# A list-scheduled order of all queues, from a first pass that notes the program as a graph, in a two-layer hybrid encoder step

## The chip, the cores and the metric

The kernel runs on one core of one Trainium2 chip. The metric is the device time of one execution in microseconds (us); less is better. Every execution starts with its inputs in the chip's memory (HBM) and ends with its outputs there. All arithmetic is in float32; the large matrix products are made of three products of float32r parts (a high and a low part of each operand), small ones are plain float32.

## What is computed

The reference is one inference step of a streaming encoder trunk with two layers on 512 prompt tokens and 32 sample tokens, 1024 features each. Cut to what matters:

```python
for layer in range(2):
    x = post_norm(x, 0.5 * swiglu(x, ffn_up[layer, 0], ffn_down[layer, 0]), ...)   # 1024 -> 2 x 2816 -> 1024
    if layer == 0:
        y, st = mixer_ab(x, ...)     # gated linear recurrence (RG-LRU) beside retention, 4 heads of 128
    else:
        y, st = mixer_c(x, ...)      # RWKV-7 time mixing, 16 heads of 64
    x = post_norm(x, y, ...)
    x = post_norm(x, cross_attn(x, mem_k[layer], mem_v[layer], xa_q[layer], xa_o[layer]), ...)  # 4 heads, 256 rows of memory
    x = post_norm(x, 0.5 * swiglu(x, ffn_up[layer, 1], ffn_down[layer, 1]), ...)
# post_norm(x, sub) = layer_norm(ALPHA * x + sub); the memory's keys and values are outputs too, and the mixers' states
```

RWKV-7's recurrence, the part that the prediction turns on, updates a 64 x 64 state of each head once per token:

```python
def step(S, inp):
    r_t, w_t, k_t, v_t, kk_t, b_t = inp
    sa = jnp.einsum('bhvk,bhk->bhv', S, -kk_t)
    S = S * w_t[:, :, None, :] + sa[..., None] * b_t[:, :, None, :] + v_t[..., None] * k_t[:, :, None, :]
    return S, jnp.einsum('bhvk,bhk->bhv', S, r_t)
```

## The kernel before

**Tiling.** The 544 tokens are two halves, A (256 prompt tokens) and B (256 prompt tokens and the 32 of the sample). A half stays in SBUF through all layers, with features on the partitions: `X` is the half itself, `XH` and `XL` its high and low parts, `HH` and `HL` those of an intermediate result (the names in the profile end in A or B). Weights come from HBM in granules of 1024 x 128 (512 KB) into one of three buffers `wr`. ScalarE makes the high part of a granule in one of five slots `W`, and VectorE or GpSimd the low part; `linear` then runs 24 matmuls of 128 x 128 weights against the half's 256 or 288 columns into one PSUM bank (`mm`). Four banks are called `mm` and four `ax`. In the feed-forward layers a granule serves both halves; from somewhat before the second layer's mixer until after its attention (`SOLO`) each half loads its own granules, so that one half's products can fill the other's waits.

**The recurrence** (`wkv` and the five tasks that it starts, in the second layer's mixer) works on nine blocks of 64 tokens (the last has 32), in chunks of 32. For every block:
- `wkv_prep` computes decays and keys. Its first instruction is a product on GpSimd (`K.gtt`, into `arena`), its second the square of that on ScalarE, its third a matmul with the matrix `bones`. It ends with a store of a triangular matrix N to HBM (`dn`).
- `wkv_solve` loads N in another layout (`P<-dn`, 512 KB, a head and chunk and a quarter of the rows to a partition), and inverts I + N in 31 steps of two GpSimd instructions (in the profile `P<-LC,P` and `LC<-LC,P`). It stores the inverse (`dz<-LC`) and loads it in a third layout (`W<-dz`), two of four loads by SP's queue and two by ScalarE's.
- `wkv_load` transposes, `wkv_chain` takes the state through the block's chunks, and `wkv_norm` norms and gates what comes out: a matmul with `cent`, four GpSimd products and sums on `HL`, and more.

**What sets the order.** Each engine takes its instructions from a queue, in order, and so does each issuer of DMAs (mostly SP; ScalarE and GpSimd for a few). The order of the queues comes about in two stages:
- A planner inside the kernel. The tasks of the program are Python generators. `Kern.run` lets go on the one that can go on first by an estimated time; each instruction passes through `Kern.plan`, and `Clock.op` says at what estimated time it starts, from durations written in the helpers (`mm`, `_v`, `gtt`, `act`, `dma`) and from when its operands are written and free. Tasks with a band under 0 (the recurrence's, the norms') see only each other's instructions as taken time; a band over 0 comes after everything. The estimated times also decide which buffer, slot or bank is taken next, and `ett` puts a subtraction on VectorE or on GpSimd, whichever the estimate has done first (the weights' low parts ask GpSimd to be 300 ns ahead).
- The framework's scheduler. `plan` hands each instruction's estimated start on as its priority. At the end the framework runs the program against its own timing model (`schedule_with_timeline_sim=True`), and whenever an engine is free in that model, the instruction of the lowest priority value among those that are ready is put next in its queue.

`place_tables` then goes through ScalarE's finished queue and puts in the loads of its function tables.

The lines that the profile names most: L395 is the matmul of `mm`, L400 the transpose of `tr`, L408 VectorE's `tt`, L412 GpSimd's `gtt`, L486 the activation of `act`, L491 the start of a DMA, L2049 a table load.

Of the kernel before, what the change touches and what calls it, by code (L numbers as in the profile page):

```python
# [3 lines left out]

# [42 lines left out]
MEM_FILL = 28  # L47
LOG_G = np.log1p(-(2.0 ** (-5.0 - np.arange(4, dtype=np.float32)))).astype(np.float32)
# [54 lines left out]
class Res:  # L103
    """Things that are taken and given back, with the times from which they are free."""
# [27 lines left out]
class Line:  # L132
    """The spans of time in which an engine is taken; a later comer may fill a gap."""
# [28 lines left out]
class Clock:  # L162
    """An estimate of when instructions run, in ns: what an engine does and what its operands wait for.
    It orders the emission and the engines' queues, and nothing else rests on it."""
# [35 lines left out]
    def renew(self, old, new):  # L200
        """A tile takes over the room of an older one."""
# [46 lines left out]

class Arena:
# [26 lines left out]
    def top(self, n):  # L276
        """The last n elements."""
# [50 lines left out]
class Arenas:  # L328
    """Several arenas as one."""
# [44 lines left out]
class Kern(Clock):  # L374
    def __init__(self, tc, ins, outs, consts, stages):
        super().__init__()
        self.tc, self.nc, self.i, self.o, self.c = tc, tc.nc, ins, outs, consts
# [6 lines left out]
    def plan(self, eng, dur, outs, ins, queue=None):  # L384
        s = self.op(eng, dur, outs, [t for t in ins if t is not None and not isinstance(t, (int, float))], self.band, queue)
        self.tc.cur_priority = 10000000 + int(s) + self.band * (BAND if self.band > 0 else 0000)

    def mm(self, out, lhsT, rhs, start=True, stop=True):
# [6 lines left out]
        self.nc.tensor.matmul(out, lhsT, rhs, start=start, stop=stop)  # L395

    def tr(self, out, in_, k0=0):
        k = in_.shape[0]
        self.plan("pe", 109.0, [out], [in_])
        self.nc.tensor.transpose(out, in_, self.ident[k0:k0 + k, k0:k0 + k])  # L400

    def _v(self, out, ins, fast=False):
        fast = fast and all(t.space != PSUM for t in ins)
        self.plan("v", 70 + free_size(out) / (1.92 if fast else 0.96), [out], ins)

    def tt(self, out, a, b, op=ALU.mult):
        self._v(out, [a, b])
        self.nc.vector.tensor_tensor(out, a, b, op=op)  # L408

    def gtt(self, out, a, b, op=ALU.mult):  # L410
        self.plan("g", 150 + free_size(out) * 2.0, [out], [a, b])
        self.nc.gpsimd.tensor_tensor(out, a, b, op=op)  # L412

    def ett(self, out, a, b, op=ALU.mult, lag=0.0):
        """On the engine that is through first; GpSimd has to be ahead by some ns."""
# [5 lines left out]
        dv, dg = 70 + n / 0.96, 150 + n * 2.0  # L421
# [8 lines left out]
    def stt(self, out, a, s, b, op0, op1):  # L430
        self._v(out, [a, b])
        self.nc.vector.scalar_tensor_tensor(out, a, s, b, op0=op0, op1=op1)  # L432

    def ts(self, out, a, s1, s2=None, op0=ALU.mult, op1=None):
        self._v(out, [a], True)
        if op1 is None:
            self.nc.vector.tensor_scalar(out, a, s1, None, op0=op0)
        else:
            self.nc.vector.tensor_scalar(out, a, s1, s2, op0=op0, op1=op1)

    def vcopy(self, out, a):
        self._v(out, [a], True)
        self.nc.vector.tensor_copy(out, a)

    def memset(self, out, v):
        self._v(out, [])
        self.nc.vector.memset(out, v)

    def gmemset(self, out, v):
        self.plan("g", 50 + free_size(out) * 0.83, [out], [])  # L450
        self.nc.gpsimd.memset(out, v)

    def scan(self, out, a, b, ini):
        self._v(out, [a, b])
        self.nc.vector.tensor_tensor_scan(out, a, b, ini, op0=ALU.mult, op1=ALU.add)

    def rmax(self, out, a):
        self._v(a, [a])
        self.nc.vector.reduce_max(out, a, axis=mybir.AxisListType.X)

    def recip(self, out, a):
        self._v(out, [a])
        self.nc.vector.reciprocal(out, a)

    def bn(self, out, tmp, a):
        self._v(a, [a])
        self.nc.vector.bn_stats(tmp, a)
        self._v(out, [tmp])
        self.nc.vector.bn_aggr(out, tmp)

    def act(self, out, a, f=AF.Copy, bias=None, scale=1.0, accum=None):
        dur = (60 if a.space == PSUM else 100) + free_size(out) / 1.2
        dur += 93 * ((bias is not None and not isinstance(bias, float)) + (not isinstance(scale, float)))
        sets = TABLES.get(f)
        if sets and self.set not in sets:
            self.set = sets[0]
            dur += 1283
        self.plan("a", dur, [out] if accum is None else [out, accum], [a])
# [7 lines left out]
        return self.nc.scalar.activation(out, a, f, bias=bias, scale=scale, **kw)  # L486

    def dma(self, out, a, queue="sync"):
        n = 4 * int(np.prod(out.shape))
        self.plan("dma", n / 350 + 60, [out], [a], queue)  # L490
        getattr(self.nc, queue).dma_start(out, a)  # L491
# [7 lines left out]
    def sigmoid(self, out, a, bias=None, half=None):  # L499
        """1 / (1 + exp(-a - bias)) = (1 + tanh((a + bias) / 2)) / 2; half: bias / 2."""  # L500
# [66 lines left out]
    def lend(self, slots, raws):  # L567
        """Slots and buffers of the weights for another use."""
# [9 lines left out]
    def stream(self, granules, after=(), limit=None, first=0):  # L578
        """Granules that are loaded one after another, from when the streams before them are through."""
# [1508 lines left out]
```

## Time and profile before

| | |
|---|---|
| time, median of 3 runs (lowest, highest) | 3021.44 us (3020.57, 3023.30) |
| the profiled execution, first to last instruction | 3028.7 us |
| TensorE busy, matmuls | 2833.4 us, 22456 |
| VectorE / ScalarE / GpSimd busy | 1743.4 / 1276.8 / 830.1 us |
| mean granted TensorE clock | 0.945 |
| from HBM, to HBM | 313.09 MB, 13.92 MB |

The profiled execution has no separate time without its profile; its span is 7.3 us over the median of the runs, and the shares of the page refer to that span. PE stands for TensorE's matmuls, PEld for its weight loads, DVE for VectorE, ACT for ScalarE, POOL for GpSimd, SP for the engine that only starts DMAs; a `q` behind a name means the engine's sequencer. A matmul's duration is longer than the distance to the next one, since matmuls are pipelined. A wait is shown with the engine that waited, its instruction, and who ended the wait.

### The profile page before, as it was taken

To read this page: it belongs to the slowest core of one execution; us is meant where nothing else is said; L and a number is where in the kernel's file an instruction comes from. 1 tells how busy PE (TensorE), PEld (TensorE's weight loads), DVE (VectorE), ACT (ScalarE), POOL (GpSimd) and SP (SyncE) were. 2 spreads that over 40 slices of the span, in tenths; PEclk is the share of its full clock that TensorE was granted. 3 is DMA by queue.
4 is the path that set the end of the run, shared out by engine and by line. 5 is a ranking of instruction groups with operands and counts; after the bars stand their busy time and mean duration, and the time that the engine had idled before them with its cause. 6 is when DMAs were issued, how large, how long until landed. Compare 5 with 4: busy or idle time off the path is not lost.

```text
span 3028.7 us, 54637 instructions
## 1 busy us (share of the span) xinstructions
PE 2833.4 (94%) x22456; PEld 2716.3 (90%) x22456; DVE 1743.4 (58%) x3099; ACT 1276.8 (42%) x2184; POOL 830.1 (27%) x1088
## 2 busy tenths in 40 slices
PE   9999998998999999999999898888878889999998
PEld 8999998998998999989999897776767779998997
DVE  5333337677767333365355756674675666767655
ACT  4223233665545222234244343343435455655544
POOL 2001104333313000032011212466375543422301
PEclk9999999999999999999999998788778879999999
DMA  6443443322332232322356453122223135645563
GB/s 182 126 119 115 130 119 97 88 68 81 98 98 84 85 90 84 89 87 77 90 155 179 120 168 106 39 65 62 69 73 87 49 98 174 177 141 157 169 176 93
DMA packets 626331, 330.56 MB, mean 109 GB/s; under 512 B 45480, under 2 KB 620160, under 8 KB 626080
## 3 DMA queue, kind: packets, MB, share of 16 engines
q1 hardware_dynamic: 617952, 317.06, 36.8%
q0 software_dynamic: 3488, 9.44, 1.0%
q8 instruction: 176, 2.88, 0.4%
q10 hardware_dynamic: 4640, 0.56, 0.1%
q14 instruction: 75, 0.61, 0.1%
HBM read 313.09 MB, written 13.92 MB: 108 GB/s over the span
## 4 chain that ended last, share of the span: by engine, by line
PE 66%; DVE 10%; POOL 9%; DMA 7%; ACT 5%; issue 3%; SPq 0%; ACTq 0%; DVEq 0%; POOLq 0%
PE mm L395 60%; PE ax L395 4%; POOL LC L412 3%; POOL P L412 3%; DMA P<-dn 3%; DVE W L408 2%; ACT arena L486 1%; ACT W L486 1%; DVE arena L408 1%; DMA wr<-in_ffn_up 1%; PE ax L400 1%; DVE arena L432 1%; POOL arena L412 1%; ACT L2049 1%; DVE XB L408 1%
## 5 line engine op out<-in xcount | busy, mean ns | idle before, releaser
L486 ACT ACTIVATE W<-wr 128x1024 fp32r<-128x1024 f32 (+1 forms) x558 | 577.0, 1038 | 737.4 <-PE mm L395 560.0
L408 DVE TENSOR_TENSOR W<-wr,W 128x1024 fp32r<-128x1024 f32 (+1 forms) x455 | 561.5, 1236 | 551.7 <-ACT W L486 542.8
L395 PE MATMUL mm<-XHB,W 128*128 128x288 f32 x3840 | 585.1, 302 | 14.1 <-ACT XHB L486 4.7
L395 PE MATMUL mm<-XHA,W 128*128 128x256 f32 x3840 | 538.4, 290 | 28.9 <-ACT XHA L486 11.6
L395 PEld LDWEIGHTS mm<-XHB,W 128*128 128x128 f32 x3840 | 532.4, 191 | 25.0 <-ACT XHB L486 5.8
L395 PEld LDWEIGHTS mm<-XHA,W 128*128 128x128 f32 x3840 | 499.7, 194 | 39.7 <-ACT XHA L486 16.0
L412 POOL TENSOR_TENSOR W<-wr,W 128x1024 fp32r<-128x1024 f32 (+1 forms) x103 | 251.0, 2439 | 606.2 <-ACT W L486 550.6
L395 PE MATMUL mm<-XLB,W 128*128 128x288 f32 x1984 | 318.7, 300 | 0.7 <-DVE XLB L408 0.7
L395 PE MATMUL mm<-HHB,W 128*128 128x288 f32 x1920 | 291.0, 301 | 11.4 <-ACT W L486 4.4
L395 PEld LDWEIGHTS mm<-XLB,W 128*128 128x128 f32 x1984 | 283.0, 190 | 3.2 <-DVE XLB L408 1.1
L395 PE MATMUL mm<-XLA,W 128*128 128x256 f32 x1984 | 284.7, 283 | 0.0
L395 PEld LDWEIGHTS mm<-HHB,W 128*128 128x128 f32 x1920 | 267.0, 191 | 15.0 <-ACT W L486 5.3
L395 PE MATMUL mm<-HHA,W 128*128 128x256 f32 x1920 | 265.7, 288 | 5.9 <-POOL W L412 2.2
L395 PEld LDWEIGHTS mm<-XLA,W 128*128 128x128 f32 x1984 | 259.1, 190 | 0.3 <-DVE XLA L408 0.2
L395 PEld LDWEIGHTS mm<-HHA,W 128*128 128x128 f32 x1920 | 247.1, 192 | 8.8 <-POOL W L412 2.6
L486 ACT ACTIVATE arena<-mm 128x256 f32<-128x256 f32 (+4 forms) x292 | 112.2, 387 | 305.1 <-PE mm L395 287.5
L432 DVE SCALAR_TENSOR_TENSOR arena<-mm,arena 128x288 f32<-128x288 f32 (+1 forms) x176 | 77.2, 439 | 157.7 <-PE mm L395 149.0
L395 PE MATMUL mm<-HLB,W 128*128 128x288 f32 x896 | 144.3, 301 | 0.3 <-DVE HLB L408 0.3
L412 POOL TENSOR_TENSOR P<-LC,P 128x66 f32<-128x66 f32 (+24 forms) x279 | 113.5, 407 | 84.6 <-DMA P<-dn 64.6
L395 PEld LDWEIGHTS mm<-HLB,W 128*128 128x128 f32 x896 | 130.1, 193 | 0.6 <-DVE HLB L408 0.5
L395 PE MATMUL mm<-HLA,W 128*128 128x256 f32 x896 | 129.3, 284 | 0.0
L412 POOL TENSOR_TENSOR LC<-LC,P 128x66 f32<-128x66 f32 (+24 forms) x279 | 115.0, 412 | 20.5
(426 smaller groups left out, 3612.0 us busy)
## 6 DMA issues: line engine op xcount, KB each, us to landing
wr<-in_ffn_up SPq DMA_DIRECT2D x246, 512.0 KB
wr<-in_ffn_down SPq DMA_DIRECT2D x96, 448.0 KB
wr<-in_l_w_rkv SPq DMA_DIRECT2D x48, 512.0 KB
wr<-in_ffn_down SPq DMA_DIRECT2D x40, 512.0 KB
wr<-in_l_w_in SPq DMA_DIRECT2D x24, 512.0 KB
wr<-in_l_w_out SPq DMA_DIRECT2D x24, 512.0 KB
wr<-in_xa_q SPq DMA_DIRECT2D x24, 512.0 KB
wr<-in_xa_o SPq DMA_DIRECT2D x24, 512.0 KB
```

Source lines behind the costliest of these rows:

```text
L395: self.nc.tensor.matmul(out, lhsT, rhs, start=start, stop=stop)
L400: self.nc.tensor.transpose(out, in_, self.ident[k0:k0 + k, k0:k0 + k])
L408: self.nc.vector.tensor_tensor(out, a, b, op=op)
L412: self.nc.gpsimd.tensor_tensor(out, a, b, op=op)
L432: self.nc.vector.scalar_tensor_tensor(out, a, s, b, op0=op0, op1=op1)
L486: return self.nc.scalar.activation(out, a, f, bias=bias, scale=scale, **kw)
L2049: nc.scalar.preload_act_table_set(name)
```

## The change

The program is built twice. In the first pass a `Graph` notes each instruction as a node: its engine, its duration, its queue, the nodes that it must wait for (by the same areas of tiles that the planner uses; a whole bank for PSUM), whether it uses the port that VectorE and GpSimd share, which tables it can run with, and its planned start. Then the first pass is thrown away, `Graph.schedule` runs a list scheduler over the nodes, and the second pass, which makes the same instructions, ties each engine's instructions to each other in the order of the starts that the scheduler found. The framework's own scheduler is off (`schedule_with_timeline_sim=False`).

- The list scheduler goes forward in time. Whenever a queue is free, it takes the ready node with the lowest planned start (the same value as the priority before). ScalarE lets a node that needs another table wait, if one that doesn't is ready and planned less than `SWAP` = 3000 ns later. A VectorE or GpSimd instruction that needs the shared port waits for it, or lets another go ahead.
- A DMA holds its queue for 50 ns (700 on GpSimd's) and lands 1300 ns, the transfers ahead of it, its own bytes / 350 + 60 ns, and 900 ns later.
- The durations in the helpers are new, for the planner too; operands that were left out of the estimates (scalars and biases) are taken in.
- Nothing else in the program changes: the computation, the tiles and the other constants of the planner stay; the engine that `ett` picks, and the buffers that come free first, follow from the new durations. Comments and docstrings are gone.

The diff, cut to its core:

```diff
+SWAP = 3000.0
+class Graph:
+    TAIL = {"pe": 175.0, "v": 25.0, "a": 25.0, "g": 25.0}
...
+    def schedule(self):
...
+        prio = self.at
...
+        while True:
+            t, l = min((max(free[m], 0.0 if now[m] else soon[m][0][0]), m) for m in names if now[m] or soon[m]) \
+                if any(now.values()) or any(soon.values()) else (None, None)
...
+            p, k = heappop(a)
+            if l == "a" and self.sets[k] and table not in self.sets[k]:
+                same = min((x for x in a if not self.sets[x[1]] or table in self.sets[x[1]]), default=None)
+                if same is not None and same[0] < p + SWAP:
...
+                    k = same[1]
+            if self.port[k] and port > t:
+                other = min((x for x in a if not self.port[x[1]]), default=None)
...
+            elif e == "dma":
+                issue = 700.0 if l == "g" else 50.0
+                free[l] = t + issue
+                if l == "g":
+                    port = max(port, t + issue)
+                dma = max(t + issue + 1300.0, dma) + d
+                end = dma + 900.0
+            else:
+                if l == "a" and self.sets[k] and table not in self.sets[k]:
+                    table = self.sets[k][0]
+                    d += 1283.0
+                free[l] = t + d
+                end = t + d + self.TAIL[e]
+                if self.port[k]:
+                    port = t + d
...
     def plan(self, eng, dur, outs, ins, queue=None, sets=None):
...
-        self.tc.cur_priority = 10000000 + int(s) + self.band * (BAND if self.band > 0 else 0000)
+        if self.graph is not None:
+            self.graph.add(self, eng, dur, outs, ins, queue, sets, s + max(self.band, 0) * BAND)
+    def chain(self):
+        info = mybir.DependencyInfo(mybir.DependencyClass.NoSync, mybir.DependencyReason.DATA)
+        last = {}
+        for _, k in sorted((t, k) for k, t in enumerate(self.starts)):
+            i = self.made[k]
+            if i.engine in last:
+                self.tc.add_manual_dep(i, last[i.engine].name, info, reason="schedule")
+            last[i.engine] = i
...
-            cost = (n if n >= 256 else max(4 * n, 128)) / 2.4 + 2
+            cost = n / 2.4 + 13 if n >= 256 else max(4 * n / 2.4, 108.0) + 2
...
-            cost = 4 * (max(n, 62) / 2.4) + 2
+            cost = max(4 * n / 2.4, 108.0) / side + 2
...
-        self.plan("v", 70 + free_size(out) / (1.92 if fast else 0.96), [out], ins)
+        self.plan("v", 147 + free_size(out) / (1.92 if fast else 0.96), [out], ins)
...
-        self.plan("g", 150 + free_size(out) * 2.0, [out], [a, b])
+        self.plan("g", 190 + free_size(out) * 2.1, [out], [a, b])
...
-        dv, dg = 70 + n / 0.96, 150 + n * 2.0
+        dv, dg = 147 + n / 0.96, 190 + n * 2.1
...
-        dur = (60 if a.space == PSUM else 100) + free_size(out) / 1.2
-        dur += 93 * ((bias is not None and not isinstance(bias, float)) + (not isinstance(scale, float)))
+        dur = (165 if a.space == PSUM else 204) + free_size(out) / 1.2
+        dur += 88 * ((bias is not None and not isinstance(bias, float)) + (not isinstance(scale, float)))
...
-    with tile.TileContext(nc, schedule_with_timeline_sim=True) as tc:
-        build(tc, ins, outs, consts, STAGES)
...
+            with tile.TileContext(nc, schedule_with_timeline_sim=False) as tc:
+                build(tc, ins, outs, consts, STAGES, graph, starts)
+                if graph is not None:
+                    raise Planned
...
+    graph = Graph()
+    program_of(graph, None)
+    at = graph.schedule()
+    nc = program_of(None, [t for e, t in zip(graph.eng, at) if e != "x"])
     place_tables(nc)
```

More of the change, by code (lines that the diff above doesn't have):

```diff
@@ L3 @@
 from contextlib import contextmanager
+from heapq import heapify, heappop, heappush
 import numpy as np
@@ L200, in renew @@
     def renew(self, old, new):
+        if old is not None and self.graph is not None:
+            self.graph.renew(self, old, new)
         if old is not None and old.tensor.name in self.cells:
@@ L249 @@
+class Planned(Exception):
+    pass
 class Arena:
@@ L381, in __init__, with plan, note, mm @@
         self.tags = {}
-    def plan(self, eng, dur, outs, ins, queue=None):
-        s = self.op(eng, dur, outs, [t for t in ins if t is not None and not isinstance(t, (int, float))], self.band, queue)
-        self.tc.cur_priority = 10000000 + int(s) + self.band * (BAND if self.band > 0 else 0000)
-    def mm(self, out, lhsT, rhs, start=True, stop=True):
+    def plan(self, eng, dur, outs, ins, queue=None, sets=None):
+        ins = [t for t in ins if t is not None and not isinstance(t, (int, float))]
+        swap = 1283 if sets and self.set not in sets else 0
+        if swap:
+            self.set = sets[0]
+        s = self.op(eng, dur + swap, outs, ins, self.band, queue)
+        if self.graph is not None:
+            self.graph.add(self, eng, dur, outs, ins, queue, sets, s + max(self.band, 0) * BAND)
+    def note(self, made):
+        self.made.append(made.ins)
+        return made
+    def chain(self):
[6 more added lines that the diff above has]
+            last[i.engine] = i
+    def mm(self, out, lhsT, rhs, start=True, stop=True, side=1):
         n = free_size(rhs)
         if lhsT.dtype == F32R:
-            cost = (n if n >= 256 else max(4 * n, 128)) / 2.4 + 2
+            cost = n / 2.4 + 13 if n >= 256 else max(4 * n / 2.4, 108.0) + 2
         else:
-            cost = 4 * (max(n, 62) / 2.4) + 2
+            cost = max(4 * n / 2.4, 108.0) / side + 2
         self.plan("pe", cost, [out], [lhsT, rhs])
-        self.nc.tensor.matmul(out, lhsT, rhs, start=start, stop=stop)
+        self.note(self.nc.tensor.matmul(out, lhsT, rhs, start=start, stop=stop))
     def tr(self, out, in_, k0=0):
@@ L468, in bn @@
+        self.note(self.nc.vector.bn_stats(tmp, a))
         self._v(out, [tmp])
-        self.nc.vector.bn_aggr(out, tmp)
+        self.note(self.nc.vector.bn_aggr(out, tmp))
     def act(self, out, a, f=AF.Copy, bias=None, scale=1.0, accum=None):
-        dur = (60 if a.space == PSUM else 100) + free_size(out) / 1.2
-        dur += 93 * ((bias is not None and not isinstance(bias, float)) + (not isinstance(scale, float)))
[L474 to L477, printed above, removed]
@@ L490, in dma @@
         self.plan("dma", n / 350 + 60, [out], [a], queue)
-        getattr(self.nc, queue).dma_start(out, a)
+        self.note(getattr(self.nc, queue).dma_start(out, a))
     def gdma(self, out, a):
@@ L696, in build @@
         K.run()
+        if starts is not None:
+            K.chain()
 VEC = {}
```

188 lines of the change are left out of this document (150 added, 38 removed).

## The prediction

> **What bounds the kernel now.** I read the page first: its busy times and its 40 slices.
>
> ```profile
> span 3028.7 us, 54637 instructions
> PE 2833.4 (94%) x22456; PEld 2716.3 (90%) x22456; DVE 1743.4 (58%) x3099; ACT 1276.8 (42%) x2184; POOL 830.1 (27%) x1088
> PE   9999998998999999999999898888878889999998
> PEclk9999999999999999999999998788778879999999
> ```
>
> TensorE is the bound by share, and no instruction goes away in this change. What an order can win is TensorE's idle time, 3028.7 - 2833.4 = 195 us, and clock that the throttle takes: slices 25 to 33 show 7 and 8 tenths. The view by windows, asked for the recurrence stage (1893 to 2498 us), for what lies before and behind it, and for one dense slice, puts numbers to that. A row gives the stretch, the busy us and counts of TensorE, its weight loads, VectorE, ScalarE and GpSimd, then clock, DMA share and GB/s.
>
> ```profile
> 1059.00:1135.00 76.00, 76.00 (x603) 76.00 (x602) 25.06 (x37) 17.70 (x26) 0.00 (x0) 1.00 0.32 91
> 0.00:1893.00 1893.00, 1815.34 (x14035) 1786.31 (x14035) 1008.83 (x1868) 739.66 (x1276) 360.74 (x332) 0.98 0.38 109
> 1893.00:2498.00 605.00, 512.61 (x4472) 434.46 (x4471) 393.96 (x727) 264.18 (x486) 335.39 (x671) 0.81 0.26 68
> 2498.00:3028.00 530.00, 505.44 (x3954) 495.49 (x3952) 340.61 (x505) 272.91 (x423) 133.93 (x86) 0.98 0.53 155
> ```
>
> The dense slice has no idle time at a clock of 1.00: 76.00 / 603 = 126 ns for a matmul. No order can shorten such a slice. The stage from 1893 is different: 605 - 512.6 = 92.4 us idle in a fifth of the span, at a clock of 0.81. Elsewhere 77.7 + 24.6 = 102.3 us are idle in 2423. So I looked for the stage's waits, TensorE's first.
>
> ```profile
> PE ax L395 <- ACT HLB L486: 14.2, 4, 9.9
> PE mm L395 <- POOL W L412: 13.2, 4, 7.3
> PE mm L395 <- DVE W L408: 12.4, 9, 2.7
> PE ax L400 <- ACT TGB L486: 7.8, 1, 7.8
> PE mm L395 <- ACT arena L486: 7.4, 1, 7.4
> PE ax L395 <- ACT HLA L486: 7.0, 1, 7.0
> PE mm L395 <- ACT XHA L486: 4.9, 2, 2.6
> ACT arena L486 <- POOL arena L412: 59.7, 8, 17.6
> ACT HLA L486 <- DMA dz<-LC: 11.0, 1, 11.0
> POOL P L412 <- DMA P<-dn: 64.6, 9, 10.7
> POOL LC L451 <- DMA dz<-LC: 38.1, 8, 5.0
> ```
>
> Each row gives the total, how often, and the longest. TensorE's long waits end with a ScalarE or GpSimd result (14.2 + 13.2 + 7.8 + 7.4 + 7.0 + 4.9 = 54.5 us), ScalarE's with GpSimd, GpSimd's with a load. The timeline of the longest case shows that these are one thing:
>
> ```profile
> 2241.62 0.24 POOL L412 TENSOR_TENSOR P<-LC,P 128x31 f32<-128x31 f32 x1 [7.81 <-DMA P<-dn]
> 2270.85 1.04 POOL L412 TENSOR_TENSOR arena<-HLB,pv 128x512 f32<-128x512 f32 x1
> 2271.92 0.63 ACT L486 ACTIVATE arena<-arena 128x512 f32<-128x512 f32 x1 [17.62 <-POOL arena L412]
> 2274.14 2.08 PE L395 MATMUL ax<-HLB,centt 128*128 128x512 f32 x2 [9.88 <-ACT HLB L486]
> 2275.38 0.70 POOL L412 TENSOR_TENSOR LC<-LC,P 128x8 f32<-128x8 f32 x1
> ```
>
> The solve's 62 steps (written P and LC) hold GpSimd from 2241.62 to 2276.08. The next block's first product, `arena<-HLB,pv`, was put among the last of them. ScalarE's queue has that product's square at its head, and stands 17.62 us with everything behind it; TensorE stands 9.88 us for the copy HLB, which isn't the square's result at all but lies behind it in ScalarE's queue. Queues are in order, and the order was fixed by a clock in which GpSimd got there much earlier. This is what the change can mend.
>
> **Part by part: the prices.** The graph's list scheduler uses the same planned times as priorities as the framework's did, so the rule of choice stays; what changes is the clock that it runs by. These rows test it:
>
> ```profile
> L486 ACT ACTIVATE W<-wr 128x1024 fp32r<-128x1024 f32 x462 | 486.5, 1056 | 548.8 <-PE mm L395 404.0 <-DMA wr<-in_ffn_up 77.2 <-issue 16.3
> L408 DVE TENSOR_TENSOR XA<-XA,mm 128x256 f32<-128x256 f32 x80 | 33.0, 415 | 25.2 <-PE mm L395 24.9
> L412 POOL TENSOR_TENSOR W<-wr,W 128x1024 fp32r<-128x1024 f32 x95 | 233.5, 2459 | 514.8 <-ACT W L486 490.9 <-issue 8.4 <-DVE XB L408 7.4
> L2049 ACT ACT_TABLE_LOAD x56 | 71.8, 1283 | 1.0
> ```
>
> New prices: ScalarE 204 + 1024/1.2 = 1057 ns (row 1056; old 953); VectorE from PSUM 147 + 256/0.96 = 414 (row 415; old 337); GpSimd 190 + 2.1 x 1024 = 2340 (row 2459; old 2198); matmul (120 + 133)/2 = 126 (slice 126; old 115). On the four engines the new clock is right to 5%. What the framework's clock charged stands in no row; its errors do, as the waits above.
>
> The choice of engine for a split compares 1214 with 2340 instead of 1137 with 2198, so some of GpSimd's 95 may go to VectorE, at 1.2 us each there. I take 0: VectorE is 58% busy; without that cover 10 moved splits would be 12 us. Table loads: 56 x 1.283 = 71.8 us, priced now, and a use that needs a change of set is held back up to 3 us of planned time. ScalarE is 42% busy, so I take 0; bounds: some 10 us either way, if held uses or saved loads all lay on the stage's path. The added operands (biases, scalars) are written early and add no wait that I can find: 0.
>
> **The queues.** DMAs are tied too: SP's loads, the pair of `W<-dz` on ScalarE's queue, the stores on GpSimd's. Here the new clock isn't measured: 50 + 1300 + bytes/350 + 60 + 900 ns, so 3.8 us for the solve's 512 KB and 2.7 us for `dz`. The chain of waits shows:
>
> ```profile
> 1900.68 9.14 DMA P<-dn
> 2071.76 12.19 DMA P<-dn
> 2119.64 4.72 DMA dz<-LC
> ```
>
> So the load is priced 5 to 8 us short and `dz` 2 us short. Behind the first solve step stand, in GpSimd's queue, the next block's product and the norm's products, and behind those ScalarE and TensorE; behind a `W<-dz` on ScalarE's queue stand the evictions (11.0 us, above). That part of the old fault remains.
>
> The rule that speaks against my reading is in the Trainium skill, "SBUF — State Buffer", section "Summary: rules for kernel authors": estimate a transfer between HBM and SBUF at about 358 GB/s. By it the graph's 350 bytes per ns would be right, and the whole of the 54.5 us could go; 512 KB in 9.14 us is 57 GB/s, so the measurement decides and the load stays short-priced.
>
> **The sum.** In the 17.62 us case 7.81 us is the late load, which stays, and 9.81 is GpSimd's pace, which the graph prices: 56%. So:
> - the stage's waits for ScalarE and GpSimd: 0.56 x 54.5 = 30 us;
> - clock: 605 us at 0.81 is 0.19 x 605 = 115 us of clock withheld, which costs only where TensorE paces. The chain of waits of the stage gives TensorE's instructions 18.3 + 5.7 + 2.1 = 26%:
>
> ```profile
> by line: PE mm L395 18.3%; POOL LC L412 14.5%; POOL P L412 14.4%; DMA P<-dn 14.1%; issue 6.2%; PE ax L395 5.7%; POOL HLA L412 3.0%; DVE W L408 2.7%; DMA dn<-W 2.5%; DMA dz<-LC 2.4%; PE ax L400 2.1%; POOL W L412 1.6%; ACT arena L486 1.2%; PO
> ```
>
> that is 30 us, and with 56% of the stalls gone I take 17 us back (bounds 0 and 30; a loss here belongs to the slower rival);
> - outside the stage most waits are a norm's data, but the filler's matmuls stand for its own copy, an order's fault:
>
> ```profile
> PE mm L395 <- DVE arena L443: 8.4, 2, 7.1
> ```
>
> 8 us (bounds: -8, since the new order may as well put another such head there, and 34, if all idle time there fell by a third).
>
> The Trainium skill ("TensorE: Matmul & The Clock Gate", section "HAM oscillation — how this bites in real kernels") has it that gaps over about 3.4 us bring the half clock. By it only the five rows with a longest wait of 7 us or more would matter, each with a window of 3.4 us at half clock: an estimate of 5 x 1.7 = 9 us instead of 17. The stage's 0.81 withholds 115 us, far more than five windows do, so the row decides.
>
> Sum: 30 + 17 + 8 = 55 us. The profiled execution spans 3028.7 us, 7.3 more than the median 3021.44 of the runs; taken off that median: **2966 us**, -1.8%. That case's own range: 2927 (30 + 30 + 34 us) to 3011 (a third of the waits, and neither of the other terms).
>
> **Rivals.** *Slower: short-priced loads.* If the framework's clock had the solve's load and `dz` nearer to 11 and 4.7 us than the graph's 3.8 and 2.7, the new order puts the solve's first step, and every product planned behind it, about 6 + 2 us too early in each block. Eight blocks x 8 us = 64 us more on ScalarE's head and TensorE; half hidden by the other half's dense products gives 32: **3054 us**; unhidden 3085. For it: the row of 38.1 us for `dz`, the load's 14.1% of the stage's chain. Against: GpSimd already waits 64.6 / 9 = 7.2 us per load, so the old clock was short as well. It decides when the wait for `P<-dn` grows above 7.2 us per block and ScalarE's wait for GpSimd above 59.7 us. Re-dealt buffers (the planner's times set which buffer comes free first) push the same way.
>
> *No change.* The stage's own chain paces it: solve, load, `dz`, next block, and the order only moves waits between engines: **3021 us**. For it: solve steps and load hold 14.5 + 14.4 + 14.1 = 43% of the chain. It is also what comes out if the tying changes little, the priorities being the same.
>
> *Much faster.* The blocks close up. The view by windows for the instructions of tile P alone (the fifth busy time is GpSimd's):
>
> ```profile
> 1893.00:2498.00 605.00, 12.26 (x120) 10.70 (x120) 4.86 (x10) 3.97 (x8) 228.53 (x558) 0.81 0.26 68
> ```
>
> There are nine blocks: 228.53 / 9 = 25.4 us of solve in each, (335.39 - 228.53) / 9 = 11.9 of other work, 9.14 load, 4.72 `dz`: 51.2 us against 605 / 9 = 67.2. Nine times 16.0 = 144: **2877 us**. Against: that work isn't all ready when GpSimd is free, and the load stays mispriced.
>
> **How the numbers follow.** Forecast 0.50, slower 0.32, no change 0.10, much faster 0.08. A difference under 0.2% (6 us) can't be told from no change here. Faster 0.50 + 0.08 = 0.58, same 0.10, slower 0.32. The two signs hold most of the chance, so the range spans them: from 2890, which leaves most of the 0.08 out, to 3062, just past the slower rival's price, which leaves about 0.12 out.
>
> **What would show it.** Right: in the changed profile ScalarE's wait for `arena` from GpSimd falls from 59.7 to about 30 us, TensorE's idle time in the stage to about 60, the stage's clock above 0.85, GpSimd's wait for `P<-dn` stays near 65, the dense slices stay at 126 ns. The loads' rival shows in that wait growing. The forecast is wrong if the stage keeps its 605 us, or if idle time shows up in slices that were full, behind a queue's tied head.

## The result and the profile after

The changed kernel takes 3125.22 us (median of 4 runs, 3112.86 to 3132.87) against 3021.01 us before (4 runs, 3018.6 to 3023.3). The ratio is 1.0335, with a 95% interval of 1.031 to 1.0361: 104 us slower. The forecast was 2966 us, and 3125 lies outside its range too. The profiled execution took 3121.91 us and spans 3120.1 us.

The page of the changed kernel, its busy times and two rows of slices:

```profile
span 3120.1 us, 54601 instructions
...
PE 2874.2 (92%) x22456; PEld 2745.5 (88%) x22456; DVE 1742.8 (56%) x3097; ACT 1295.2 (42%) x2191; POOL 801.9 (26%) x1090
...
PE   8999999998998999989999996889887688999998
...
PEclk9999999998999999999999997789778678999999
```

TensorE runs the same 22456 matmuls. It is busy for 40.8 us longer (2874.2 - 2833.4) and idle for 50.6 us longer (245.9 against 195.3); together that is the 91.4 us by which the span grew. The view by windows says where (stretch, then busy us and counts of TensorE, weight loads, VectorE, ScalarE and GpSimd, then clock, DMA share, GB/s):

```profile
1000.00:1076.00 76.00, 76.00 (x604) 76.00 (x604) 26.53 (x39) 19.08 (x30) 0.00 (x0) 1.00 0.31 88
0.00:1893.00 1893.00, 1807.67 (x13920) 1778.65 (x13921) 963.72 (x1815) 741.05 (x1264) 338.47 (x324) 0.98 0.37 108
1893.00:2600.00 707.00, 573.45 (x4763) 482.90 (x4761) 441.25 (x785) 287.63 (x519) 350.78 (x689) 0.78 0.25 66
2600.00:3120.10 520.10, 493.12 (x3776) 483.96 (x3776) 337.81 (x498) 266.50 (x410) 112.63 (x77) 0.97 0.52 153
```

The dense slice still runs at 76.00 / 604 = 126 ns a matmul. The recurrence stage takes the loss: its idle time went from 92.4 to 707 - 573.45 = 133.6 us and its clock from 0.81 to 0.78. Outside it the idle time went from 102.3 to 85.3 + 27.0 = 112.3 us.

The last step of the last solve marks the end of that stage. It is the row `LC<-LC,P` of 128x8 on GpSimd, first in the kernel before, then in the changed one:

```profile
2474.32 0.21 POOL L412 TENSOR_TENSOR LC<-LC,P 128x8 f32<-128x8 f32 x1
```

```profile
2580.29 1.22 POOL L592 TENSOR_TENSOR HLB<-HLB,gng 128x512 f32<-128x512 f32 x1
2581.47 0.21 POOL L592 TENSOR_TENSOR LC<-LC,P 128x8 f32<-128x8 f32 x1
2581.63 1.26 POOL L592 TENSOR_TENSOR HLB<-HLB,HHB 128x512 f32<-128x512 f32 x1
```

It comes 107 us later, and in the changed order it stands between products of the norm. Of the 107 us, 28 are a later first step of the first solve (1938.1 against 1909.9) and 86 are longer solves: the mean of the nine, first step to last, grew from 35.1 to 44.6 us. The gaps between solves add up to 7 us less than before (241.9 against 248.8).

The waits of the changed kernel in 1893 to 2600 (total, times, longest) answer to those shown of before:

```profile
POOL LC L631 <- DMA dz<-LC: 58.4, 8, 12.0
POOL P L592 <- DMA P<-dn: 52.6, 7, 15.7
...
ACT arena L662 <- PE ax L574: 42.9, 27, 4.6
...
ACT arena L662 <- POOL arena L592: 30.2, 9, 12.0
...
PE ax L574 <- DMA W<-dz: 19.2, 5, 10.5
...
PE mm L574 <- DVE W L623: 12.7, 4, 9.9
...
PE mm L574 <- POOL W L592: 10.3, 6, 2.7
...
PE ax L574 <- ACT XB L662: 9.8, 1, 9.8
...
PE mm L574 <- ACT W L662: 9.5, 11, 1.5
...
PE mm L574 <- ACT arena L662: 8.1, 6, 3.3
...
PE mm L574 <- ACT XHA L662: 3.5, 1, 3.5
...
PE ax L574 <- ACT HLA L662: 3.1, 3, 1.2
...
PE ax L574 <- ACT HLB L662: 1.9, 2, 1.2
```

The stall that the prediction chose did shrink: ScalarE's wait for `arena` from GpSimd fell from 59.7 to 30.2 us. But TensorE waits longer than before. If all of its rows in 1893 to 2600 are added up by what ended them, for both kernels, the sum is 94.6 us before (ScalarE 49.6, VectorE 31.0, GpSimd 13.2, DMA 0.8) and 132.5 after (ScalarE 52.9, VectorE 47.9, DMA 21.4, GpSimd 10.3). The longest wait in the DMA rows, in the timeline:

```profile
2465.43 0.54 SPq L667 DMA_DIRECT2D P<-dn  x1
2466.02 0.54 SPq L667 DMA_DIRECT2D dz<-LC  x1
...
2477.21 0.91 ACTq L667 DMA_DIRECT2D W<-dz  x2
2477.25 0.82 SPq L667 DMA_DIRECT2D W<-dz  x2
2477.30 0.90 POOL L631 MEMSET LC<- 128x256 f32 x5 [11.61 <-DMA dz<-LC]
2478.17 0.42 ACT L662 ACTIVATE arena<-XA 128x256 f32<-128x256 f32 x1 [6.82 <-DMA dz<-LC]
2478.28 2.34 POOL L592 TENSOR_TENSOR W<-wr,W 128x1024 fp32r<-128x1024 f32 x1
2478.61 2.29 DVE L588 TENSOR_TENSOR arena<-arena 128x256 f32<-128x256 f32 x1 [5.77 <-ACT arena L662]
2480.15 1.94 PE L574 MATMUL ax<-arena,W 128*128 128x64 f32 x8 [10.46 <-DMA W<-dz]
```

SP issues the next block's load just ahead of this block's store `dz`. The store, issued at 2466.02, lands some 11 us later (the `W<-dz` that wait for it go out at 2477.2), where the row of before had 4.72. Five queues stand at their heads for that one store: SP and ScalarE with `W<-dz`, GpSimd for 11.61 us, VectorE behind ScalarE for 5.77, TensorE for 10.46.

The chain of waits through the stage, by line, in the changed kernel:

```profile
by line: PE mm L574 35.5%; PE ax L574 17.4%; PE ax L579 4.9%; issue 3.3%; DMA dz<-LC 3.2%; ACT W L662 2.7%; POOL LC L592 2.4%; POOL W L592 2.3%; POOL P L592 2.2%; DVE W L588 2.1%; ACT arena L662 2.0%; DMA W<-dz 1.7%; DMA HLB<-in_l_a 1.6%; D
```

Before, TensorE held 26% of this chain and the solve's steps with the load 43%. Now TensorE holds 35.5 + 17.4 + 4.9 = 58%, and the two rows of solve steps 4.6%. With the same matmuls to do, the chain now runs mostly through TensorE's queue, and at a lower clock.

### The profile page after: what moved, and what is told of

Its sections match the earlier page's. It is cut to its first block, busy times and chain, and to the rows that moved or that the text cites. A ratio compares the mean times of both kernels' runs of the same rounds, so it can differ in the third digit from the quotient of the medians.

```text
span 3120.1 us, 54601 instructions
## 1 busy us (share of the span) xinstructions
PE 2874.2 (92%) x22456; PEld 2745.5 (88%) x22456; DVE 1742.8 (56%) x3097; ACT 1295.2 (42%) x2191; POOL 801.9 (26%) x1090
## 4 chain that ended last, share of the span: by engine, by line
PE 80%; DVE 6%; DMA 4%; ACT 4%; POOL 3%; issue 2%; SPq 0%; ACTq 0%; POOLq 0%; DVEq 0%
PE mm L574 71%; PE ax L574 7%; PE ax L579 2%; ACT W L662 1%; DVE W L588 1%; ACT arena L662 1%; POOL W L592 1%; DMA dz<-LC 1%; DMA wr<-in_ffn_up 1%; DVE XB L588 1%; DVE XA L588 1%; POOL LC L592 1%; DMA wr<-in_l_w_rkv 1%; POOL P L592 0%; DVE arena L588 0%
## 5 line engine op out<-in xcount | busy, mean ns | idle before, releaser
L574 PE MATMUL mm<-XHA,W 128*128 128x256 f32 x3840 | 540.5, 293 | 50.6 <-ACT XHA L662 26.0
L574 PEld LDWEIGHTS mm<-XHA,W 128*128 128x128 f32 x3840 | 503.8, 196 | 60.0 <-ACT XHA L662 27.6
L592 POOL TENSOR_TENSOR W<-wr,W 128x1024 fp32r<-128x1024 f32 (+1 forms) x99 | 236.7, 2392 | 877.1 <-ACT W L662 769.0
L574 PE MATMUL mm<-HHA,W 128*128 128x256 f32 x1920 | 272.5, 292 | 13.4 <-ACT arena L662 3.5
L592 POOL TENSOR_TENSOR P<-LC,P 128x66 f32<-128x66 f32 (+24 forms) x279 | 110.4, 396 | 71.9 <-DMA P<-dn 52.6
L574 PEld LDWEIGHTS mm<-HLA,W 128*128 128x128 f32 x896 | 119.2, 193 | 1.4 <-issue 1.0
```

The lines of the kernel that those rows point to most:

```text
L574: self.note(self.nc.tensor.matmul(out, lhsT, rhs, start=start, stop=stop))
L592: self.note(self.nc.gpsimd.tensor_tensor(out, a, b, op=op))
```

## The experiments

Eighteen kernels were run. "Last solve" is the end of the last solve's last step in the profiled run, "idle" is span less TensorE's busy time, "clock" the mean granted clock. The ratio is to the kernel before on the same chip.

| run | median us | ratio (95%) | last solve | span | idle | clock |
|---|---|---|---|---|---|---|
| before | 3021.01 | 1 | 2474.5 | 3028.7 | 195.3 | 0.945 |
| jitter_before | 3033.97 | 1.0041 (1.0028 to 1.0054) | 2467.4 | 3029.9 | 210.9 | 0.947 |
| scale_before | 3037.71 | 1.0041 (1.0026 to 1.0056) | 2470.6 | 3036.1 | 198.5 | 0.940 |
| prices_only | 3071.25 | 1.0151 (1.0136 to 1.0166) | 2502.7 | 3065.5 | 233.9 | 0.937 |
| all_priced_no_port | 3092.03 | 1.0213 (1.0189 to 1.0236) | 2541.5 | 3093.9 | 207.0 | 0.934 |
| no_port_rule | 3104.2 | 1.0255 (1.0239 to 1.0272) | 2549.5 | 3102.3 | 231.1 | 0.938 |
| clock_priced | 3104.3 | 1.0258 (1.024 to 1.0275) | 2560.2 | 3105.6 | 238.4 | 0.937 |
| scale_after | 3118.08 | 1.0312 (1.0288 to 1.0337) | 2584.1 | 3116.5 | 248.1 | 0.933 |
| recurrence_first | 3118.66 | 1.0318 (1.0301 to 1.0336) | 2576.0 | 3113.9 | 262.7 | 0.933 |
| after | 3125.22 | 1.0335 (1.031 to 1.0361) | 2581.7 | 3120.1 | 245.9 | 0.932 |
| graph_old_prices | 3125.99 | 1.0337 (1.0319 to 1.0354) | 2578.8 | 3122.7 | 224.9 | 0.926 |
| dma_priced | 3126.91 | 1.0327 (1.031 to 1.0345) | 2589.0 | 3127.3 | 257.4 | 0.931 |
| tie_pool | 3128.37 | 1.0347 (1.033 to 1.0365) | 2589.7 | 3126.3 | 278.3 | 0.926 |
| tail0 | 3134.05 | 1.0373 (1.0335 to 1.0411) | 2591.3 | 3154.1 | 252.6 | 0.923 |
| jitter_after | 3136.68 | 1.0371 (1.0338 to 1.0403) | 2608.7 | 3144.3 | 257.1 | 0.927 |
| all_priced | 3151.26 | 1.0414 (1.0397 to 1.0432) | 2575.4 | 3144.8 | 234.0 | 0.925 |
| order_only | 3171.29 | 1.0484 (1.0462 to 1.0506) | 2623.2 | 3168.3 | 265.1 | 0.922 |
| tie_act_sp | 3182.07 | 1.0533 (1.05 to 1.0566) | 2630.1 | 3178.9 | 299.2 | 0.924 |
| tie_dve | 3228.07 | 1.0674 (1.0653 to 1.0695) | 2675.2 | 3230.8 | 345.9 | 0.919 |
| tie_pe | 3269.96 | 1.0809 (1.0792 to 1.0827) | 2721.8 | 3267.6 | 348.7 | 0.909 |

One thing holds in all twenty traces. Span less last solve lies between 532 and 569 us, while the last solve itself moves by 254 us, from 2467 to 2722. So the end of the last solve is a good mark of what an order is worth here. It is a mark and not yet a cause: in the changed kernel the solve's own steps hold little of the chain that leads there.

### Prices or order: four combinations

**prices_only** keeps the new prices and operands of the planner, and lets the framework order the queues as before:

```
-            with tile.TileContext(nc, schedule_with_timeline_sim=False) as tc:
+            with tile.TileContext(nc, schedule_with_timeline_sim=True) as tc:
...
+        self.tc.cur_priority = 10000000 + int(s) + self.band * (BAND if self.band > 0 else 0000)
...
-    graph = Graph()
-    program_of(graph, None)
-    at = graph.schedule()
-    nc = program_of(None, [t for e, t in zip(graph.eng, at) if e != "x"])
+    nc = program_of(None, None)
```

> The new prices of the planner and the added operands, but the queues ordered as before by the framework's own timing model: no graph and no tie. If the loss of 104 us comes from the graph's order and its tie, this run stands within 15 us of the kernel before, 3021. If it comes from the planner's new prices, which re-deal buffers, the choice of engine and the priorities, it stands above 3080.

**order_only** gives the planner the prices of before and the graph the new ones:

```
-        s = self.op(eng, dur + swap, outs, ins, self.band, queue)
+        s = self.op(eng, od + swap, oo, oi, self.band, queue)
```

(`od`, `oo`, `oi` are the old price and operands of the same instruction.)

> The planner keeps the kernel before's prices, so buffers, engines and priorities are those of before; the graph has its measured durations and ties every queue. If the order and its tie cost the time, this run stands near 3125, within 20. If the planner's new prices do, it stands near 3021.

**graph_old_prices** lets the graph run by the old prices too:

```
-            self.graph.add(self, eng, dur, outs, ins, queue, sets, s + max(self.band, 0) * BAND)
+            self.graph.add(self, eng, od, outs, ins, queue, sets, s + max(self.band, 0) * BAND)
```

> The run with the order alone (old planner, graph with measured durations, all queues tied: 3171), but the graph too runs by the planner's old, shorter prices. If the measured durations are what makes the tied order worse, as the planner's new prices alone cost 45 us, this falls below 3110. If the list scheduler's rule, its port and the tie cost it whatever the prices, it stays within 20 us of 3171.

Measured: 3071, 3171 and 3126, and none of the three stands where either side of its expectation had it. Both parts of the change cost time alone. By the framework's order the planner's new prices cost 1.5% (45 us). By the graph's order it makes no difference whether planner and graph both use old prices (3126) or both new ones (3125), and a mixture is worst (3171). So the order costs 101 us at the old prices (3125.99 against 3024.6 of before in the same series) and 54 at the new. Lower prices in the graph took 45 us from the mixture (not to below 3110, as expected) and left the tied order 101 us above the framework's, so what makes it worse is not that its durations are longer. These runs change the durations in the helpers alone: the framework's own timing model and the graph's rule for DMAs are the same in all of them.

The chain of the stage under the framework's order and the new prices (1893 to 2510) looks like that of before, with GpSimd's solve first and TensorE at 20%:

```profile
by line: POOL P L593 15.9%; POOL LC L593 15.8%; PE mm L575 13.6%; DMA P<-dn 11.4%; issue 7.0%; PE ax L575 6.2%; DMA dz<-LC 6.1%; DMA dn<-W 2.1%; DVE W L589 1.9%; POOL HLB L593 1.5%; DVE arena L613 1.4%; ACT W L663 1.3%; POOL HLA L593 1.3%; 
```

With the old planner and the tied order (1893 to 2630) it looks like that of the changed kernel, TensorE at 29.8 + 21.2 + 4.2 = 55%:

```profile
by line: PE mm L579 29.8%; PE ax L579 21.2%; DMA dz<-LC 4.2%; PE ax L584 4.2%; issue 4.0%; ACT arena L674 3.4%; DVE W L597 3.0%; ACT W L674 2.8%; POOL W L601 2.7%; POOL LC L601 2.7%; POOL P L601 2.2%; DMA wr<-in_xa_o 1.3%; POOL HLB L601 1.3
```

So the chain's move to TensorE's queue comes with the graph's order, and not with the planner's new prices. It is not the whole of the loss, though. In the run without the port rule (below; 1893 to 2570) TensorE holds 19.8 + 8.9 + 2.1 = 31% and the solve's steps with the load 42%, much as before the change, and that run is still 2.6% slower than the kernel before:

```profile
by line: PE mm L574 19.8%; POOL LC L592 15.9%; POOL P L592 15.3%; DMA P<-dn 10.7%; PE ax L574 8.9%; issue 7.7%; DMA dz<-LC 4.8%; PE ax L579 2.1%; DVE W L588 1.9%; POOL W L592 1.8%; POOL HLB L592 1.8%; DMA dn<-W 1.2%; POOL HLA L592 0.8%; SPq
```

### What the graph lacks: transfers, holes, half clock, port

**dma_priced**, the slower rival's own cause:

```
-                end = dma + 900.0
+                end = dma + 900.0 + self.late.get(k, 0.0)
...
-            K.dma(N, dn[None].to_broadcast([4, m, 32, 32]))
+            K.dma(N, dn[None].to_broadcast([4, m, 32, 32]), late=5400.0)
-            K.dma(dz, Z)
+            K.dma(dz, Z, late=2200.0)
```

> The changed kernel with two numbers of its graph mended: the solve's load lands 5.4 us later (9.2 instead of 3.8) and the store of the solved block 2.2 us later. Theory 1, short-priced loads: GpSimd's waits in the middle of a solve, some 67 us, mostly go, a solve takes about 36 us instead of 44.6, and the time falls to 3040 to 3060. If the loads are not the cause, it stays between 3105 and 3135.

3127 us: nothing came back. The stage's waits in that kernel (1893 to 2600) show that the two prices did act:

```profile
POOL LC L633 <- DMA dz<-LC: 52.9, 6, 12.9
ACT arena L664 <- POOL arena L594: 33.7, 8, 14.8
POOL P L594 <- DMA P<-dn: 26.1, 3, 20.6
...
PE mm L576 <- ACT XHA L664: 17.0, 3, 11.0
PE mm L576 <- DVE W L625: 13.0, 4, 8.1
PE ax L581 <- DVE arena L619: 10.5, 3, 7.2
...
PE ax L576 <- DMA W<-dz: 0.3, 1, 0.3
```

GpSimd's wait for the load halved (52.6 to 26.1) and TensorE's for `W<-dz` went (19.2 to 0.3), but TensorE now waits for ScalarE and VectorE instead, and the last solve ends no earlier. The rival's waits are real, and removing these two did not change the time. GpSimd's wait for `dz` stays (58.4 to 52.9): the plan still issues a load right ahead of a store once, and that store again lands some 11 us after its issue, where the new price has 4.9.

**tail0** closes the holes between dependent instructions of one engine, in which the graph puts other work between two steps of a solve:

```
-                if e == "pe" and eng[j] == "pe" and self.bank[k] == self.bank[j]:
+                if e == eng[j] and (e in "vag" or e == "pe" and self.bank[k] == self.bank[j]):
```

> The changed kernel, but in the graph an instruction that needs the result of the one before it on the same engine is ready when that one ends, not 25 ns after, so that other work no longer slips in between two steps of the solve. Theory 2, holes: a solve takes about 35 us as before instead of 44.6, and nine times 9.5 us come back: about 3040. By theory 1 the solves get shorter, but the waits move to the work behind them, and the time stays above 3090.

3134 us. The mean solve fell from 44.6 to 32.5 us, shorter than before the change, and the time did not fall. What was taken out of the nine solves (109 us) came back between them: the gaps from one solve's end to the next one's start add up to 362.5 us instead of 241.9, and the longest is 113 us (58 in the changed kernel, 64 before).

**no_port_rule** and **clock_priced**:

```
-        port = eng == "g" or (eng == "v" and len(ins) > 0 and all(t.space != PSUM for t in ins))
+        port = False
```

> The changed kernel, but its graph lets GpSimd and VectorE run at the same time (the rule that keeps them apart when VectorE reads only SBUF is off). Theory 3, the rule is too strict: on the chip they mostly overlap, the rule spreads the planned work for nothing, and without it the time falls to 2960 to 2990. Rival: the rule is right, the plan without it is too dense, and the queues tied to it stand at their heads: 3150 to 3200.

```
+                if e == "pe":
+                    while w < int(t / WIN):
+                        slow = used.get(w, 0.0) < (0.9 if slow else 0.5) * WIN
+                        w += 1
+                    if slow:
+                        d *= 2
+                    used[w] = used.get(w, 0.0) + min(d, (w + 1) * WIN - t)
...
```

> The changed kernel, but its graph prices a matmul double in a window of 3.41 us that follows one in which TensorE was busy less than half (until one is busy 0.9), as the records of granted clock show it in the profile of the kernel before and of the changed one. Theory 4, the half clock is what the plan lacks: 35 to 65 of the 104 us come back, 3060 to 3090. By the other theories no change: 3110 to 3140.

Each stands at 3104, 21 us below the changed kernel, between the two sides of its expectation. The port rule's result needs a second look, because the exclusion that it models is real. In the timeline above VectorE's `arena<-arena` takes 2.29 us where this shape takes 0.42 alone, and it ends at 2480.90, right behind the weight split on GpSimd that ends at 2480.62. It is no single case: in the trace of the changed kernel `HLB<-arena,HHB` of 128x288, with both inputs in SBUF, took 2.42 us in the median where a GpSimd instruction was in flight at its start (17 times) and 0.45 alone (74), while `XB<-XB,mm` of the same shape, with one input in PSUM, took 0.45 either way (25 and 50). The Trainium skill ("SBUF — State Buffer", section "Who interferes with whom") says that a VectorE instruction with two inputs in SBUF contends with a GpSimd instruction that reads SBUF, over a pair of ports that is an exclusive lock; the trace agrees. So a plan without the rule is not faster because the engines overlap. Here a clock that is truer in this point made no better order.

**all_priced** (half clock, transfers and holes) and **all_priced_no_port** (half clock and transfers, port rule off):

> The changed kernel with three things priced at once: the half clock as in the run before, the solve's load 5.4 us and the solved block's store 2.2 us later, and no 25 ns between dependent instructions of one engine. If the loss is a sum of prices that the graph lacks, this is the best of the tied orders, 3055 to 3080, but still over the kernel before, 3021. If the loss lies in the list scheduler's rule or in the tie itself, it stays above 3100.

> The half clock and the two transfers priced, and the port rule off. Theory 3 with theory 4: 2930 to 2960, faster than the kernel before. If the port rule is right: 3150 to 3190.

3151 and 3092. The first, expected to be the best of the tied orders, is slower than the changed kernel although its graph knows three more things; the second, far from either side of its expectation, is the best tied order, 33 us under the changed kernel and still 2.1% over the kernel before. Its page:

```profile
span 3093.9 us, 54624 instructions
...
PE 2886.9 (93%) x22456; PEld 2754.4 (89%) x22456; DVE 1763.5 (57%) x3097; ACT 1293.5 (42%) x2190; POOL 812.2 (26%) x1090
...
PEclk9999999899999999999999898786888679999999
```

TensorE's idle time, 207.0 us, is nearly that of before (195.3). The rest is 53.5 us of busy time. By the mean clocks 0.066 x 3093.9 = 204 us of clock are withheld against 0.055 x 3028.7 = 167 before, so half clock can account for some 37 of the 53.5; the remainder is not explained.

### One queue at a time

With the planner of before, the graph's order was put on some queues alone, and the framework ordered the rest around it:

```
             i = self.made[k]
+            if str(i.engine).split(".")[-1] not in TIED:
+                continue
```

> The planner's old prices and the graph as in the run with the order alone (3171, where the same planner under the framework's order is the kernel before, 3026), but only TensorE's queue is tied to the graph's order; the framework's timing model orders the other four around it. If TensorE's own order holds most of the 145 us, this stands above 3100; if it is another queue's, below 3050.

> As the run before, but only VectorE's queue is tied. Theory 5, filler first: the list scheduler takes whatever is ready, so the other half's residual adds and splits stand ahead of the recurrence's products on VectorE, and this queue alone brings most of the 145 us: above 3100. If the order on VectorE is harmless, below 3050.

> Only ScalarE's queue and SP's are tied, loads and evictions. If the loads' places are what costs, above 3100; by theory 5 little, 3025 to 3060.

> Only GpSimd's queue is tied: the solve, its neighbours and the stores. If the work put in between the solve's steps is what costs, above 3100; by theory 5 less than VectorE's, 3040 to 3080.

Each costs time alone: 246 us for TensorE, 204 for VectorE, 158 for ScalarE with SP, 104 for GpSimd (before, in the same series: 3024.0), against 145 for all of them together. The expectations by theory 5, little for ScalarE with SP and 3040 to 3080 for GpSimd, failed. The four runs were after one guilty queue and don't show one. TensorE's or VectorE's order from one plan and the rest from another is worse than either plan; the mixture with GpSimd's order stands between the two. So this way of testing can't split the 145 us.

### Is it the order, or any other order?

**jitter_before** and **jitter_after** move each priority by at most 150 ns; **scale_before** and **scale_after** make every planned duration 1% longer (the second diff is that of scale_before; in scale_after `dur` is scaled in the planner and in the graph):

```
+        self.count += 1
+        s += (self.count + 1) * 2654435761 % 4294967296 / 4294967296 * 300 - 150
```

```
-        s = self.op(eng, dur + swap, outs, ins, self.band, queue)
+        s = self.op(eng, 1.01 * dur + swap, outs, ins, self.band, queue)
```

> The kernel before, its planner and its framework's order, but each instruction's priority is moved by a fixed pseudo-random amount of at most 150 ns, about one matmul. Theory 6, the order of before is one selected draw and any other costs: 3040 to 3080. Rival, the graph's rule is worse by itself and neighbouring orders are alike: within 10 us of 3025.

> The kernel before with every duration of its planner 1% longer, nothing else: as good a clock as before, but buffers, engines and priorities are dealt anew. Theory 6: 3040 to 3090, like the 3071 of the new prices. Rival: within 10 us of 3025.

> The changed kernel with its graph's priorities moved by the same amounts of at most 150 ns. Theory 6: it moves by 10 to 40 us either way from 3125, so that steps of 21 us between tied orders say little. Rival: within 10 us of 3125.

> The changed kernel with every duration of its planner and its graph 1% longer. Theory 6: it moves by 10 to 50 us either way from 3125. Rival: within 10 us of 3125.

Neighbours of the kernel before stand 0.4% above it (12 us), neighbours of the changed kernel 12 us above and 7 below. So the loss isn't the price of any new draw: its neighbours share it. It is also a measure for the rest. The two neighbours of the changed kernel stand 19 us apart, so the two runs at 21 us below it can hardly be read. The 33 us of all_priced_no_port are more than that, but it is the best of several tied orders, so part of them may be luck.

### The recurrence first

**recurrence_first**:

```
-            self.graph.add(self, eng, dur, outs, ins, queue, sets, s + max(self.band, 0) * BAND)
+            self.graph.add(self, eng, dur, outs, ins, queue, sets, s + max(self.band, 0) * BAND - (100000.0 if self.band < 0 else 0.0))
```

> The changed kernel, but in its graph every instruction of the recurrence's five tasks goes ahead of any other that is ready (its planned time less 100 us). Theory 5, filler first: the last solve ends some 40 to 60 us earlier than 2582 and the time falls by as much, to 3065 to 3085. Rival, the holes are left by the recurrence's own chain of steps and not by who goes first: within 15 us of 3125.

3119 us, inside the rival's margin. The edit goes by the band, so it moves up the norms' instructions too, which have a band under 0 as well. The first solve did start earlier (1907 instead of 1938 us), and the last ended at 2576.0 instead of 2581.7. That the filler is taken ahead of the recurrence does not explain the loss.

## Why the prediction was wrong, point by point

**The bound** was read rightly: the dense slices kept their 126 ns, and all that moved lies in TensorE's idle time and clock.

**The stall that was to go** changed its name. Its mark, ScalarE's wait for `arena`, was foretold at about 30 us and is 30.2. The six rows that made 54.5 us now make 1.9 + 10.3 + 0 + 8.1 + 3.1 + 3.5 = 26.9, 27.6 us less, where 30 were forecast. But other rows came in their place, such as the 9.8 us for `XB` and the 9.5 for `W` from ScalarE. All of TensorE's waits that ScalarE or GpSimd ended (1893 to 2600) make 49.6 + 13.2 = 62.8 us before and 52.9 + 10.3 = 63.2 after, so the term of 30 us brought nothing. That the mark and the six rows fell by the foretold size is therefore no proof of the reason given, and the 56% were weakly founded: the late load had landed at 2241.62, 12.7 us before the wait of 17.62 us began (2271.92 - 17.62 = 2254.30), so it was no part of that wait.

**The step that failed** is the sentence ahead of the prices: "the rule of choice stays; what changes is the clock that it runs by." The whole sum rests on it: old stalls were counted as errors of a clock, and a better clock was to take them away from an order that otherwise stayed. The order did not stay. With the planner's old prices in both cases, the tied order takes 3126 us and the framework's 3025, a loss of 101 us from the exchange of schedulers. Truer durations did not help either: by the graph, old prices give 3126 us and new ones 3125, and by the framework's order the planner's new prices made it 45 us worse. The prices were right to 5%, and that bought nothing. What in the exchange costs the time, the graph's rules or what its clock still lacks against the framework's, these runs don't separate.

**The waits that the new order makes** have no term in the sum. TensorE's waits in the stage rose from 94.6 to 132.5 us: for DMA from 0.8 to 21.4, for VectorE from 31.0 to 47.9, for ScalarE from 49.6 to 52.9 in spite of the rows that fell. TensorE's idle time in the stage was to fall to about 60 us and rose to 133.6.

**The clock term** has the wrong sign. Of the stage, 605 x 0.19 = 115 us of clock were withheld before, 707 x 0.22 = 156 after; 17 us back and a clock above 0.85 were forecast. The bound below nothing was given to the slower rival, and the rival's price didn't hold it either.

**The filler term** of 8 us: outside the stage the idle time grew by 10 us, a little past the bound of -8.

**Terms at nothing.** The table loads were taken at 0 within 10 us:

```profile
L2229 ACT ACT_TABLE_LOAD x63 | 80.8, 1283 | 1.1
```

There are 63 for 56, 9.0 us more, on an engine that is 42% busy. Some splits did move from GpSimd to VectorE: with the smaller shape counted in, GpSimd's group holds 99 instead of 103 and VectorE's 459 instead of 455. Four at about 1.2 us each are some 5 us on VectorE, which is 56% busy; whether they or the table loads cost time was not tested.

**The slower rival** had the sign right and not the cause. Its marks were a growing wait for `P<-dn` (it fell, 64.6 to 52.6) and for `arena` (it halved); `dz` did grow, 38.1 to 58.4. Pricing both transfers moved the waits and left the time.

**What stays open.** The loss sits in the order that the graph's scheduler makes of the recurrence stage: in the changed kernel the nine solves take 86 us longer, the last one ends 107 us later, and the stage's chain runs mostly through TensorE's queue. The two transfers' prices, the holes, the level of the prices and the recurrence's rank, each mended alone, gave nothing back. The half clock and the port rule, with the transfers, may be worth some 33 of the 104 us together. Why the framework's order, made by a clock that no run shows, ends the solves earlier is not settled by these runs. Three rivals are untested: the rule that holds a node back for ScalarE's tables (`SWAP`), a store's place behind a load on SP's queue, and the graph's starts handed to the framework as priorities, which would part the clock from the rule of choice. No run compares the starts that the graph planned with those of the trace. That a plan without slack passes each delay on to every queue that is tied to it would fit the runs, but was only argued.

## What to carry to other kernels

When a change replaces the scheduler and its prices at once, measure the four combinations first; here each half alone cost time, and a truer price list was worth nothing. A new order of in-order queues makes waits of its own, so a forecast needs a term for them, and a stall counts as gone only when the sum of the engine's waits falls: here six chosen rows fell by 27.6 us and the sum of the waits for the same two engines not at all. Find an event that the end follows (here the last solve, with 532 to 569 us behind it in twenty traces) and ask of a change whether it comes earlier, before counting waits.

## What the runs showed of the hardware

A store of 128 KB issued 0.6 us behind a 512 KB load on the same queue landed some 11 us after its issue, where one by itself took 4.72. The same pair occurs once each in five more traces (order_only, dma_priced, tail0, all_priced and jitter_after), and there the load that waits for the store goes out 10.9 to 12.3 us after the store's issue.

The granted clock is recorded in windows of 3.41 us, each at 1.0 or at 0.5. The kernel before has 98 of them at half clock, the changed one 124: half of 98 x 3.41 is 167 us and half of 124 x 3.41 is 211 us, which agrees with the mean clocks (0.055 x 3028.7 = 167 and 0.068 x 3120.1 = 212). So the 0.81 of the stage is made of whole windows. The Trainium skill ("TensorE: Matmul & The Clock Gate", section "HAM oscillation — how this bites in real kernels") puts such switches down to idle gaps of over about 3.4 us. The trace agrees with the length of 3.4 us and not with gaps of that length as the only cause: TensorE has 12 gaps over 3.4 us before and 11 after, and the clock went down 36 and 43 times. In the kernel before TensorE was busy for 0.34 of the window ahead of such a change in the median, and for under 0.5 in 28 of the 36. The other way round, no full-clock window with a busy share under 0.47 was followed by another at full clock, in either trace, and the clock came back only after a window that was busy for 0.84 or more. So short gaps that add up go with the change too; no run here isolated them as its cause.
